# A transformer and state-space layer in float32 halves: the high and low parts of the activations side by side in memory, and one 512-column matmul for both

## The chip, the cores and the metric

The kernel runs on one core of a Trainium2 chip. The metric is the device time of one execution in microseconds (us), as the median of three runs. One further execution was recorded by the hardware profiler; all rows in this document that carry durations come from such recorded executions. TensorE (PE) does the matmuls, and its weight loads are listed apart (PEld); VectorE is DVE, ScalarE is ACT, SyncE (SP) issues nearly all transfers.

## The reference, cut to what matters

One layer for 256 tokens of width 1024, all in float32. Two feed-forward half steps enclose a mixer of latent attention and a state-space part:

```
x = x + 0.5 * swiglu(rmsnorm(x, ffn1_norm), w_gate1, w_up1, w_down1)     # inner width 2816
u = rmsnorm(x, mix_norm) @ w_in
c_q, c_kv, k_pe, z, xbc, dt_f, dt_b, g_a, g_b = split(u)
a = mla(c_q, c_kv, k_pe, ...)
m = bi_mamba2(xbc, z, dt_f, dt_b, ...)
merged = sigmoid(g_a) * (a @ w_attn_branch) + sigmoid(g_b) * (m @ w_ssm_branch)
x = x + merged @ w_out
x = x + 0.5 * swiglu(rmsnorm(x, ffn2_norm), w_gate2, w_up2, w_down2)

swiglu(h, wg, wu, wd) = (silu(h @ wg) * (h @ wu)) @ wd
```

## The kernel before, in words

Everything is kept transposed: 128 features on the partitions, the 256 tokens along the free dimension. A weight matrix is cut into tiles of 128 by 128; one such tile of the inner dimension is called a k-tile here.

**Three products for one.** Large products run on numbers of the reduced type fp32r, and accuracy is kept by splitting each operand into a high part and a low part: x = xh + xl, w = whi + wlo. `wstat` (line 140) goes over the k-tiles and calls `mm3` (lines 135 to 138) for each, which issues whi with xh, whi with xl and wlo with xh, all three into the same 256 PSUM columns. Each of these matmuls has a weight load of its own in the trace, so a k-tile takes three weight loads and three matmuls of 256 columns. The high parts and the low parts of the activations lie in separate tiles (`xh`, `xl`, `hh`, `hl`, `ah`, `al`, `mh`, `ml`, `oh`, `ol`).

**Weights.** `wload` (line 112) fetches a piece of up to 1088 columns into one of four raw buffers (pool `raw`), lets ACT make the high part by a copy (line 121 through line 94) and DVE the low part by a subtraction (line 122 through line 97), into one of four buffers each (pool `w`). The split carries a raised priority (`WPRI`). The order of instructions on each engine is laid down when the program is built, by a list scheduler that goes by such priorities and by its own estimate of when operands are there; the queues then run strictly in that order.

**Feed forward** (`ffn`, line 237). For each of 22 blocks f of the inner width, 1 MB of weights comes in as two pieces (gate and up), 16 k-tiles are multiplied into one PSUM bank, `gu` is the bank times the norm row R (line 264, DVE, straight from PSUM), ACT takes the silu of the gate half (266), DVE multiplies it with the up half (267), and `split` makes `hh` and `hl` of the result (268, one ACT and one DVE instruction). The PSUM pool has six one-bank buffers. Then come 8 down tiles d of 22 k-tiles each, with four pieces of weights; one DVE instruction (274) adds half of the 256 columns to x; `after(d)` feeds the next norm or, in the second half step, sends out a tile of the output. During blocks 8 to 18 of the first half step the hook also fetches and splits six pieces of the mixer's first weights, and during block 3 the rotary tables are made.

**Mixer.** Four rounds, in which the units of attention (`attn_group`), of the state-space part (`ssd_group`) and of weight-heavy filling are interleaved by a plan of keys (`put`). Filling is the input projection of the next group (`in_group`), in round 2 also `branch(0, c)` (first half of w_ssm_branch, copied to `mpb` by ACT), and in the last round `gates(c)`: 8 units, each two output tiles of 8 k-tiles in one PSUM bank, copied to `gt` by ACT. After the plan come the attention branch, `branch(1, c)` (added to `mpb` by DVE) and the output projection.

Of the kernel before, what the change touches and what calls it, by code (L numbers as in the profile page):

```python
# [15 lines left out]
P = 128  # L16
T = 256
# [6 lines left out]
# pool depths  # L24
# [48 lines left out]
def build(ctx, tc, A, out, dbg=None):  # L73
# [61 lines left out]
    def mm3(ps, whi, wlo, xhi, xlo, first, last):  # L135
        TE.matmul(ps, whi, xhi, start=first, stop=False)  # L136
        TE.matmul(ps, whi, xlo, start=False, stop=False)  # L137
        TE.matmul(ps, wlo, xhi, start=False, stop=last)  # L138

    def wstat(ps, pieces, xh, xl, k0, first, last):  # L140
        """ps[feature, token] += sum over the k tiles held in pieces"""
        ks = [(pc, j) for pc, j0, n in pieces for j in range(j0, j0 + n)]
        for i, (pc, j) in enumerate(ks):
            mm3(ps, pc.hi[:, j * P:(j + 1) * P], pc.lo[:, j * P:(j + 1) * P],
                xh[:, k0 + i], xl[:, k0 + i], first and i == 0, last and i == len(ks) - 1)

    def rsqrt(y, v, n):
        """y = v ** -0.5 on [P, n]"""
# [28 lines left out]
    def token_sums(psp, sq, tag):  # L177
        """[token, 2]: the sum of sq[feature, token] over its features"""
# [5 lines left out]
    def token_rows(psp, r, tag):  # L184
        """[P, token]: r[token, 2] on every partition"""
# [14 lines left out]
    def xn_tiles():  # L200
        xh = xnp.tile([P, KD, T], F32R, tag="xh", name="xh")
        xl = xnp.tile([P, KD, T], F32R, tag="xl", name="xl")
        return xh, xl

    class Norm:
        """x * gain of each tile of x as it comes, and the sum of squares"""

        def __init__(self, vcol):
            self.xh, self.xl = xn_tiles()
# [8 lines left out]
        def scale(self, k):  # L218
            g = vec[:, self.vcol + k:self.vcol + k + 1]
            split(self.xh[:, k], self.xl[:, k], x[:, k], g)  # L220
# [16 lines left out]
    def ffn(norm, wgu, wd, after, hook=None):  # L237
        with ExitStack() as es:
            hp = es.enter_context(pool("h", reuse_waits="tile"))
            ev = es.enter_context(pool("ev", 3, reuse_waits="tile"))  # L240
            ps_mm = es.enter_context(pool("ps_f", 6, space=PSUM, reuse_waits="tile"))
            ps_r = es.enter_context(pool("ps_fr", 2, space=PSUM, reuse_waits="tile"))
            hh = hp.tile([P, KF, T], F32R, name="hh")
            hl = hp.tile([P, KF, T], F32R, name="hl")
            R = None
            for f in range(KF):
                ps = ps_mm.tile([P, 2, T], F32, tag="mm", name="ps_gu")
                if f == 0 and hook:
# [4 lines left out]
                    for j in range(2):  # L253
                        wstat(ps[:, j], [(pcs[2 * j], 0, 4), (pcs[2 * j + 1], 0, 4)], norm.xh, norm.xl, 0, True, True)
# [9 lines left out]
                tt(gu, ps, R.unsqueeze(1).to_broadcast([P, 2, T]), ALU.mult)  # L264
# [3 lines left out]
                split(hh[:, f], hl[:, f], sg)  # L268
# [623 lines left out]
```

## Time and profile before

| what | us |
|---|---|
| three runs | 819.92, 818.7, 819.84 |
| median | 819.84 |
| span of the profiled execution | 817.6 |
| first half step, gate and up blocks | about 7 to 140 |
| first half step, down tiles | about 140 to 203 |
| mixer, branches, output projection | about 203 to 622 |
| second half step, gate and up blocks | about 622 to 752 |
| second half step, down tiles | about 752 to 817.6 |

The span runs from the first to the last instruction of the profiled execution; the median of the unprofiled runs lies 2.24 us above it. A matmul's listed duration is its whole way through the array, and matmuls overlap; what one costs in a row of them is the distance from its start to the next start. The granted TensorE clock was 1.00 throughout.

### The profile page before, as it was taken

The numbers are of one execution on the slowest core, as the hardware profiler recorded it, in microseconds if no ns is written. First come the engines' busy times: TensorE is split into PE (matmuls) and PEld (weight loads), VectorE is DVE, ScalarE is ACT, GpSimd is POOL, SyncE is SP. The second block draws the span as 40 slices with busy tenths as digits, with TensorE's granted clock in tenths as the row PEclk, the third lists the DMA queues.
The fourth block names the chain that finished last, engine by engine and source line by source line (L and its number), as shares of the span: only waits on it lengthen the run. The fifth ranks groups of instructions, "written<-read, shape, count | busy, mean of one in ns | idle before, by whom it ended". The sixth has DMA issues, their size and how long they took to land.

```text
span 817.6 us, 16082 instructions
## 1 busy us (share of the span) xinstructions
PE 797.8 (98%) x6480; PEld 768.8 (94%) x6480; DVE 590.3 (72%) x1192; ACT 470.2 (58%) x810; POOL 0.2 (0%) x4
## 2 busy tenths in 40 slices
PE   6999999999998999999999999999999999999998
PEld 5999999999998998988989999999999999999998
DVE  6977776566797986897897578657787766666543
ACT  6755554455367659679676666557455544444342
POOL 0000000000000000000000000000000000000000
PEclk9999999999999999999999999999999999999999
DMA  7667774667235443322325414342665555554772
GB/s 259 214 212 224 222 229 136 184 184 215 63 92 171 131 131 104 106 79 92 103 85 168 154 52 154 112 146 68 223 184 178 175 184 182 185 184 131 197 206 75
DMA packets 39098, 126.61 MB, mean 155 GB/s; under 512 B 4464, under 2 KB 5872, under 8 KB 39024
## 3 DMA queue, kind: packets, MB, share of 16 engines
q1 hardware_dynamic: 38592, 124.69, 48.7%
q8 instruction: 51, 0.84, 0.4%
q10 hardware_dynamic: 432, 0.89, 0.3%
q14 instruction: 23, 0.19, 0.1%
HBM read 124.52 MB, written 1.05 MB: 154 GB/s over the span
## 4 chain that ended last, share of the span: by engine, by line
PE 86%; DVE 6%; ACT 5%; DMA 2%; issue 1%; ACTq 0%
PE ps_gu L137 10%; PE ps_gu L138 10%; PE ps_gu L136 10%; PE ps_d L136 5%; PE ps_d L137 5%; PE ps_d L138 5%; PE ps_in L137 4%; PE ps_in L138 4%; PE ps_in L136 4%; PE ps_y L690 3%; PE ps_sb L138 2%; PE ps_sb L137 2%; PE ps_sb L136 2%; PE ps_sc L603 2%; PE ps_gt L137 1%; PE ps_o L630 1%
## 5 line engine op out<-in xcount | busy, mean ns | idle before, releaser
L94 ACT ACTIVATE whi<-raw 128x1024 fp32r<-128x1024 f32 (+4 forms) x256 | 251.3, 986 | 209.0 <-PE ps_d L137 53.1
L97 DVE TENSOR_TENSOR wlo<-raw,whi 128x1024 fp32r<-128x1024 f32 (+4 forms) x256 | 289.8, 1134 | 112.1 <-ACT whi L94 111.2
L136 PE MATMUL ps_gu<-xh,whi 128*128 128x256 f32 x704 | 201.0, 285 | 7.9 <-ACT whi L94 7.9
L137 PE MATMUL ps_gu<-xl,whi 128*128 128x256 f32 x704 | 201.2, 286 | 0.5 <-DVE xl L100 0.4
L138 PE MATMUL ps_gu<-xh,wlo 128*128 128x256 f32 x704 | 200.8, 285 | 0.0
L136 PEld LDWEIGHTS ps_gu<-xh,whi 128*128 128x128 f32 x704 | 136.5, 194 | 8.2 <-ACT whi L94 8.2
L137 PEld LDWEIGHTS ps_gu<-xl,whi 128*128 128x128 f32 x704 | 136.5, 194 | 1.0 <-DVE xl L100 0.9
L138 PEld LDWEIGHTS ps_gu<-xh,wlo 128*128 128x128 f32 x704 | 136.4, 194 | 0.5 <-DVE wlo L97 0.5
L137 PE MATMUL ps_in<-xl,whi 128*128 128x256 f32 x368 | 105.3, 286 | 0.1
L138 PE MATMUL ps_in<-xh,wlo 128*128 128x256 f32 x368 | 105.0, 285 | 0.0
L136 PE MATMUL ps_in<-xh,whi 128*128 128x256 f32 x368 | 104.4, 284 | 0.0
L137 PE MATMUL ps_d<-hl,whi 128*128 128x256 f32 x352 | 99.1, 281 | 0.0
L136 PE MATMUL ps_d<-hh,whi 128*128 128x256 f32 x352 | 99.1, 281 | 0.0
L138 PE MATMUL ps_d<-hh,wlo 128*128 128x256 f32 x352 | 99.0, 281 | 0.0
L137 PEld LDWEIGHTS ps_in<-xl,whi 128*128 128x128 f32 x368 | 70.1, 191 | 0.6 <-DVE xl L100 0.3
L138 PEld LDWEIGHTS ps_in<-xh,wlo 128*128 128x128 f32 x368 | 70.1, 191 | 0.5 <-issue 0.3
L136 PEld LDWEIGHTS ps_in<-xh,whi 128*128 128x128 f32 x368 | 70.1, 191 | 0.1
L136 PEld LDWEIGHTS ps_d<-hh,whi 128*128 128x128 f32 x352 | 66.3, 188 | 0.0
L137 PEld LDWEIGHTS ps_d<-hl,whi 128*128 128x128 f32 x352 | 66.3, 188 | 0.0
L138 PEld LDWEIGHTS ps_d<-hh,wlo 128*128 128x128 f32 x352 | 66.3, 188 | 0.0
L100 DVE SCALAR_TENSOR_TENSOR xz<-ps_in,vec,xz 128x254 f32<-128x254 f32 (+1 forms) x96 | 44.8, 476 | 1.6 <-ACT xz L520 0.9
L94 ACT ACTIVATE hh<-sg 128x256 fp32r<-128x256 f32 x44 | 18.1, 415 | 45.9 <-DVE sg L97 45.9
(222 smaller groups left out, 1467.5 us busy)
## 6 DMA issues: line engine op xcount, KB each, us to landing
raw<-in_w_gu SPq DMA_DIRECT2D x86, 512.0 KB, 4.5
raw<-in_w_in SPq DMA_DIRECT2D x62, 512.0 KB, 4.4
raw<-in_w_d SPq DMA_DIRECT2D x32, 384.0 KB, 3.2
raw<-in_w_d SPq DMA_DIRECT2D x32, 320.0 KB, 3.4
raw<-in_w_sb SPq DMA_DIRECT2D x16, 512.0 KB, 4.4
raw<-in_w_qkv SPq DMA_DIRECT2D x8, 544.0 KB, 3.8
raw<-in_w_ab SPq DMA_DIRECT2D x8, 512.0 KB, 3.8
raw<-in_w_o SPq DMA_DIRECT2D x8, 512.0 KB, 4.2
```

What stands on the lines that cost most here:

```text
L94: S.activation(dst, src, AF.Copy, scale=scale)
L97: V.tensor_tensor(out=dst, in0=a, in1=b, op=op)
L100: V.scalar_tensor_tensor(out=dst, in0=a, scalar=s, in1=b, op0=op0, op1=op1)
L136: TE.matmul(ps, whi, xhi, start=first, stop=False)
L137: TE.matmul(ps, whi, xlo, start=False, stop=False)
L138: TE.matmul(ps, wlo, xhi, start=False, stop=last)
L603: TE.matmul(sc[:, t * T:(t + 1) * T], qk[:HD, t * P:(t + 1) * P], qk[:HD, T:2 * T], start=True, stop=True)
L630: TE.matmul(po[64 * j:64 * j + 64, :T], kv[:, kt, HG * NOPE + hh_ * 64:HG * NOPE + (hh_ + 1) * 64], st[hh_][:, kt], start=kt == 0, stop=kt ...
L690: TE.matmul(py[64 * j:64 * j + 64, a:b], st[c, d][:, hh_], M[i][:, j, a:b], start=n == 0, stop=n == 3)
```

## The change

The high and the low part of an activation tile now lie side by side in one tile, `[P, K, 2, T]`, so that 512 neighbouring columns hold both (`xs`, `hs`, `as_`, `ms`, `os_`). A second function `wstat2` issues two matmuls for a k-tile: wlo with xh into the first 256 columns, and whi with both parts into all 512 columns. The products with xh (and wlo) thus gather in one half of a PSUM bank and the products of whi with xl in the other half, and the two halves are added afterwards. `wstat2` is used in both half steps (gate, up and down), in `gates` and in `branch(0, c)`. All other products keep `wstat` with three matmuls and only read the new layout.

The gate and up blocks get PSUM buffers of two banks, and the pool has three of them in place of six of one bank. The evacuation of a block is one ACT copy of the low halves, one DVE add from PSUM, and the multiplication by R, now from the copied tile. A down tile uses one bank of such a buffer, and x takes its two halves by two DVE instructions. `gates` and `branch(0, c)` use one bank for each output tile and add the halves with an ACT copy and a DVE add each. Comments were removed as well.

```diff
-    def mm3(ps, whi, wlo, xhi, xlo, first, last):
-        TE.matmul(ps, whi, xhi, start=first, stop=False)
-        TE.matmul(ps, whi, xlo, start=False, stop=False)
-        TE.matmul(ps, wlo, xhi, start=False, stop=last)
...
+    def wstat(ps, pieces, xs, k0, first, last):
+
         ks = [(pc, j) for pc, j0, n in pieces for j in range(j0, j0 + n)]
         for i, (pc, j) in enumerate(ks):
...
+            w = slice(j * P, (j + 1) * P)
+            xh, xl = xs[:, k0 + i, 0], xs[:, k0 + i, 1]
+            TE.matmul(ps, pc.hi[:, w], xh, start=first and i == 0, stop=False)
+            TE.matmul(ps, pc.hi[:, w], xl, start=False, stop=False)
+            TE.matmul(ps, pc.lo[:, w], xh, start=False, stop=last and i == len(ks) - 1)
+
+    def wstat2(ps, pieces, xs, k0, first, last):
+
+
+        ks = [(pc, j) for pc, j0, n in pieces for j in range(j0, j0 + n)]
+        for i, (pc, j) in enumerate(ks):
+            w = slice(j * P, (j + 1) * P)
+            a, b = first and i == 0, last and i == len(ks) - 1
+            if not a:
+                TE.matmul(ps[:, 0], pc.lo[:, w], xs[:, k0 + i, 0], start=False, stop=False)
+            TE.matmul(ps, pc.hi[:, w], xs[:, k0 + i], start=a, stop=b)
+            if a:
+                TE.matmul(ps[:, 0], pc.lo[:, w], xs[:, k0 + i, 0], start=False, stop=False)
...
     def xn_tiles():
-        xh = xnp.tile([P, KD, T], F32R, tag="xh", name="xh")
-        xl = xnp.tile([P, KD, T], F32R, tag="xl", name="xl")
-        return xh, xl
+        return xnp.tile([P, KD, 2, T], F32R, tag="xs", name="xs")
...
-            ps_mm = es.enter_context(pool("ps_f", 6, space=PSUM, reuse_waits="tile"))
+            ps_mm = es.enter_context(pool("ps_f", 3, space=PSUM, reuse_waits="tile"))
             ps_r = es.enter_context(pool("ps_fr", 2, space=PSUM, reuse_waits="tile"))
-            hh = hp.tile([P, KF, T], F32R, name="hh")
-            hl = hp.tile([P, KF, T], F32R, name="hl")
+            hs = hp.tile([P, KF, 2, T], F32R, name="hs")
             R = None
             for f in range(KF):
-                ps = ps_mm.tile([P, 2, T], F32, tag="mm", name="ps_gu")
+                ps = ps_mm.tile([P, 2, 2, T], F32, tag="mm", name="ps_gu")
...
-                        wstat(ps[:, j], [(pcs[j], 0, KD)], norm.xh, norm.xl, 0, True, True)
+                        wstat2(ps[:, j], [(pcs[j], 0, KD)], norm.xs, 0, True, True)
...
                 gu = ev.tile([P, 2, T], F32, tag="gu", name="gu")
-                tt(gu, ps, R.unsqueeze(1).to_broadcast([P, 2, T]), ALU.mult)
+                copy(gu, ps[:, :, 1])
+                tt(gu, ps[:, :, 0], gu, ALU.add)
+                tt(gu, gu, R.unsqueeze(1).to_broadcast([P, 2, T]), ALU.mult)
...
             for d in range(KD):
-                ps = ps_mm.tile([P, 2, T], F32, tag="mm", name="ps_d")
+                ps = ps_mm.tile([P, 2, 2, T], F32, tag="mm", name="ps_d")[:, 0]
                 for c in range(2):
                     pcs = wload(wd[d, c], [768, 640])
-                    wstat(ps[:, 0], [(pcs[0], 0, 6), (pcs[1], 0, 5)], hh, hl, 11 * c, c == 0, c == 1)
-                stt(x[:, d], ps[:, 0], 0.5, x[:, d], ALU.mult, ALU.add)
+                    wstat2(ps, [(pcs[0], 0, 6), (pcs[1], 0, 5)], hs, 11 * c, c == 0, c == 1)
+                for i in range(2):
+                    stt(x[:, d], ps[:, i], 0.5, x[:, d], ALU.mult, ALU.add)
                 after(d)
...
         def branch(b, c):
             pcs = wload(A["w_sb"][b, c], [1024, 1024])
+            if b == 0:
+                return halves(mpb[:, 2 * c:2 * c + 2], pcs, ms)
...
-            if b == 0:
-                copy(d, ps)
-            else:
-                tt(d, d, ps, ALU.add)
+            tt(d, d, ps, ALU.add)
+
+        def halves(dst, pcs, xs):
+            for j in range(2):
+                ps = ps_mm.tile([P, 2, T], F32, tag="mm", name="ps_half")
+                wstat2(ps, [(pcs[j], 0, 8)], xs, 0, True, True)
+                copy(dst[:, j], ps[:, 1])
+                tt(dst[:, j], ps[:, 0], dst[:, j], ALU.add)
...
         def gates(c):
             gt[c] = ss.tile([P, 2, T], F32, tag="xz", name="gt", bufs=10)
             pcs = wload(A["w_in2"][c], [1024, 1024])
-            ps = ps_mm.tile([P, 2, T], F32, tag="mm", name="ps_gt")
-            for j in range(2):
-                wstat(ps[:, j], [(pcs[j], 0, KD)], xh, xl, 0, True, True)
-            copy(gt[c], ps)
+            halves(gt[c], pcs, xs)
```

More of the change, by code (lines that the diff above doesn't have):

```diff
@@ L133, in split @@
             stt(lo, src, scale, hi, ALU.mult, ALU.subtract)
-    def mm3(ps, whi, wlo, xhi, xlo, first, last):
[L136 to L140, printed above, removed]
+    def wstat(ps, pieces, xs, k0, first, last):
         ks = [(pc, j) for pc, j0, n in pieces for j in range(j0, j0 + n)]
         for i, (pc, j) in enumerate(ks):
-            mm3(ps, pc.hi[:, j * P:(j + 1) * P], pc.lo[:, j * P:(j + 1) * P],
-                xh[:, k0 + i], xl[:, k0 + i], first and i == 0, last and i == len(ks) - 1)
+            w = slice(j * P, (j + 1) * P)
[13 more added lines that the diff above has]
+                TE.matmul(ps[:, 0], pc.lo[:, w], xs[:, k0 + i, 0], start=False, stop=False)
     def rsqrt(y, v, n):
@@ L253, in ffn @@
                     for j in range(2):
-                        wstat(ps[:, j], [(pcs[2 * j], 0, 4), (pcs[2 * j + 1], 0, 4)], norm.xh, norm.xl, 0, True, True)
+                        wstat2(ps[:, j], [(pcs[2 * j], 0, 4), (pcs[2 * j + 1], 0, 4)], norm.xs, 0, True, True)
                 else:
@@ L396, in build @@
         ss = es.enter_context(pool("ssd", reuse_waits="tile", side="right"))
-        xh, xl = xn_tiles()
+        xs = xn_tiles()
         for k in range(KD):
@@ L494, in build @@
         dump("acs", acs)
-        ah, al = xn_tiles()
-        mh = mp.tile([P, 8, T], F32R, name="mh")
-        ml = mp.tile([P, 8, T], F32R, name="ml")
+        as_ = xn_tiles()
+        ms = mp.tile([P, 8, 2, T], F32R, name="ms")
         mpb = mp.tile([P, 8, T], F32, name="mpb")
```

26 lines of the change are left out of this document (13 added, 13 removed).

## The prediction

> **What bounds the kernel now.** I read the page first: shares of the engines, chain of waits, costliest groups.
>
> ```profile
> span 817.6 us, 16082 instructions
> ...
> PE 797.8 (98%) x6480; PEld 768.8 (94%) x6480; DVE 590.3 (72%) x1192; ACT 470.2 (58%) x810; POOL 0.2 (0%) x4
> ...
> PE 86%; DVE 6%; ACT 5%; DMA 2%; issue 1%; ACTq 0%
> ...
> L136 PE MATMUL ps_gu<-xh,whi 128*128 128x256 f32 x704 | 201.0, 285 | 7.9 <-ACT whi L94 7.9
> ...
> L136 PEld LDWEIGHTS ps_gu<-xh,whi 128*128 128x128 f32 x704 | 136.5, 194 | 8.2 <-ACT whi L94 8.2
> ```
>
> The chain that ended last runs over PE for 86% of the span, and there are as many weight loads as matmuls. The listed 285 ns is a matmul's whole way through the array: 6480 of them would make 1847 us, so matmuls overlap. What counts is the distance between starts. The windows by stage give it:
>
> ```profile
> 7.00:32.00 25.00, 24.05 (x163) 22.89 (x164) 22.77 (x75) 17.82 (x32) 0.00 (x0) 1.00 0.82 274
> 32.00:90.00 58.00, 58.00 (x486) 58.00 (x485) 44.97 (x61) 34.58 (x50) 0.00 (x0) 1.00 0.64 206
> 90.00:140.00 50.00, 50.00 (x419) 50.00 (x418) 35.50 (x47) 25.58 (x37) 0.00 (x0) 1.00 0.64 197
> 140.00:202.60 62.60, 62.60 (x530) 62.60 (x529) 38.06 (x55) 31.80 (x48) 0.00 (x0) 1.00 0.66 191
> 450.00:485.00 35.00, 34.98 (x282) 32.12 (x282) 20.04 (x54) 24.28 (x55) 0.00 (x0) 1.00 0.31 101
> 634.00:700.00 66.00, 66.00 (x552) 65.97 (x551) 45.25 (x60) 32.87 (x49) 0.00 (x0) 1.00 0.56 180
> 700.00:752.00 52.00, 52.00 (x435) 52.00 (x435) 34.35 (x46) 24.22 (x37) 0.00 (x0) 1.00 0.55 166
> ```
>
> Columns: length, then busy time and count of PE, PEld, DVE, ACT, POOL, then clock, DMA share, GB/s. In the second half step's gate and up blocks a matmul starts every 66.00/552 = 119.6 ns, in the down tiles every 62.60/530 = 118.1 ns, without a gap. PE sets the pace there, at the full clock. In the first 25 us it does not: 163 matmuls need 153 ns each, and DVE is busy 22.77 of the 25 us.
>
> **What a k-tile costs, before and after.** Why 119.6 ns for 256 columns? Three other shapes, from the PE timeline:
>
> ```profile
> 26.18 0.61 PE L181 MATMUL ps_sum<-ones,nacc 128*128 128x1 f32 x4
> 26.64 0.36 PE L137 MATMUL ps_gu<-xl,whi 128*128 128x256 f32 x1
> ...
> 255.41 0.28 PE L555 MATMUL ps_qkv<-whi,cql 128*128 128x192 f32 x1
> 255.52 0.31 PE L558 MATMUL ps_qkv<-whi,ckh 128*128 128x256 f32 x1
> ...
> 351.55 1.03 PE L646 MATMUL ps_cb<-xz 128*128 128x256 f32 x4
> 352.41 1.04 PE L654 MATMUL ps_xT<-cst,xz 128*128 128x128 f32 x8
> 353.29 0.29 PE L597 MATMUL ps_qkT<-cst,qs 128*96 128x128 f32 x1
> ```
>
> One-column matmuls with a 128-column weight load start every 0.46/4 = 115 ns, 192-column ones after 0.11 us, the 128-column transposes every 0.88/8 = 110 ns. Below 192 columns the length of the matmul does not matter: the weight load of about 110 ns does. At 256 columns load and stream are about equal, and together cost 119.6. The row ps_cb is the other case: full float32 operands, 0.86/4 = 215 ns for 256 columns, hence a matmul twice as long under which its weight load vanishes.
>
> After the change a k-tile is one 256-column matmul, under which the next (high) weights are loaded, and one 512-column matmul, under which the next low weights are loaded. The first is today's pair: 119.6 ns (118.1 in the down tiles). No 512-column matmul is in the trace. The nearest rows bound it: 215 ns from ps_cb, and 2 x 119.6 = 239 ns if the columns themselves, not the load, made 119.6. I take 216, since at 192 columns the stream was still hidden in 110 ns and ps_cb shows a long stream losing nothing to its load. So a k-tile goes from 3 x 119.6 = 358.8 to 335.6 ns, 23.2 saved; in the down tiles from 354.3 to 334.1, 20.2 saved.
>
> The Trainium skill, page "TensorE: Matmul & The Clock Gate", section "Back-to-back issue gap", speaks for another value: it states a sustained 81 ns per matmul for 128 columns and 131 ns for 512, with weight loads pipelined between. Here 128 columns took 110 ns, so its first figure does not hold in this trace. By its second a k-tile would be an estimated 251 ns and the change worth five times as much; it is the last rival below.
>
> **Part by part**, as savings against the 817.6 us span.
>
> *Down tiles.* 2 x 8 x 22 = 352 k-tiles x 20.2 ns = 7.1 us. DVE is busy 38.06 of 62.60 us there; eight more additions are covered by its idle time.
>
> *Gate and up, second half step.* 352 k-tiles x 23.2 = 8.2 us, if DVE keeps up: PE's block of 16 k-tiles goes from 5.74 to 5.37 us. What is added to a block, by the nearest groups:
>
> ```profile
> L97 DVE TENSOR_TENSOR gu<-ps_gu,R 128x512 f32<-128x512 f32 x44 | 30.2, 689 | 17.2 <-PE ps_gu L138 17.2
> L97 DVE TENSOR_TENSOR E<-E,cb 128x512 f32<-128x512 f32 x48 | 32.1, 686 | 1.8 <-ACT E L681 1.4
> L94 ACT ACTIVATE gt<-ps_gt 128x512 f32<-128x512 f32 x8 | 4.7, 588 | 0.1
> L100 DVE SCALAR_TENSOR_TENSOR x<-ps_d,x 128x256 f32<-128x256 f32 x16 | 6.8, 424 | 6.8 <-PE ps_d L138 6.4
> L97 DVE TENSOR_TENSOR yg<-yg,xz 128x256 f32<-128x256 f32 x16 | 6.7, 418 | 0.1
> ```
>
> The add takes the place of today's multiplication from PSUM (689 ns); the multiplication from SBUF is new on DVE (like E<-E,cb, 686 ns) and the copy is new on ACT (like gt<-ps_gt, 588 ns). How DVE works through a block when it need not wait for PE:
>
> ```profile
> 89.61 0.68 DVE L97 TENSOR_TENSOR gu<-ps_gu,R 128x512 f32<-128x512 f32 x1
> 90.21 1.22 DVE L97 TENSOR_TENSOR wlo<-raw,whi 128x1024 fp32r<-128x1024 f32 x1
> 91.34 0.42 DVE L97 TENSOR_TENSOR sg<-sg,gu 128x256 f32<-128x256 f32 x1
> 92.25 0.42 DVE L97 TENSOR_TENSOR hl<-sg,hh 128x256 fp32r<-128x256 f32 x1 [0.48 <-ACT hh L94]
> 93.20 1.22 DVE L97 TENSOR_TENSOR wlo<-raw,whi 128x1024 fp32r<-128x1024 f32 x1 [0.53 <-ACT whi L94]
> 94.34 0.68 DVE L97 TENSOR_TENSOR gu<-ps_gu,R 128x512 f32<-128x512 f32 x1
> ```
>
> Start to start 94.34 - 89.61 = 4.73 us, of which 1.01 are waits for ACT. The new multiplication adds 0.60 (gu to the next start, 90.21 - 89.61): 5.33 us, against PE's 5.37. If other work fills the waits it is 4.32; if DVE also waits out the copy each time, 4.73 + 0.60 + 0.59 = 5.92. Since ACT has the room (32.87 busy of 66.00, plus 0.59 a block), and a block waits for nothing that PE holds back for over one block (four weight buffers, three PSUM buffers), I take the 5.33: it just fits. Saving 7.8 of the 8.2. Should DVE lag, its queue holds behind the waiting add the next wlo and so PE's weights.
>
> *Gate and up, first half step.* The same 8.2, but DVE has more to do here. Busy 22.77 + 44.97 + 35.50 = 103.2 us in 133; 22 new multiplications make it 116.4, while PE could be done in 124.8. That leaves 8.4 us for waits; at 1.01 for the 17 blocks after the start there are 17. Ends: nothing lost (8.2), or all waits kept (116.4 + 17 + 2.2 of the start = 135.6, 2.6 slower than now). In the first 25 us, 163/3 = 54 k-tiles, nothing is to be gained (1.3 us). The order is laid out anew, and where DVE is late more work lies ready to fill a wait, so I go a little above the middle: 3.0 saved.
>
> *Mixer.* gates: 8 x 16 = 128 k-tiles x 23.2 = 3.0 us; branch(0, c): 4 x 16 = 64 x 23.2 = 1.5. Each of the 24 output tiles adds a DVE addition of 0.42 (yg row), and the ACT copy is cut in two; in 450 to 485 DVE is busy 20.04 of 35 us and ACT 24.28, which covers it. Attention and state-space units cross these stages, so I take 3.5, ends 2 and 4.5.
>
> *Ends.* After the last matmul two additions stand in line for x where there was one: 0.4 us at the end of the kernel, and 0.4 before the mixer's first norm tile, which PE waits for (0 if hidden). Lost: 0.8.
>
> *Nothing for the rest.* Weight bytes are the same; 1 MB per 5.37 us is 195 GB/s, and the first window moved 274. Three PSUM pairs hold a block each, and a pair is free about 1.3 us (copy and add) after its last matmul, two blocks before it is needed. Other products keep their three matmuls.
>
> Sum: 7.1 + 7.8 + 3.0 + 3.5 - 0.8 = 20.6 us. Span 797.0; the runs' median is 819.84, 2.24 above the span, and I carry that along: **799.2 us**.
>
> **Rivals.**
>
> *DVE takes over the gate and up blocks* (the other side). The copy stands on ACT behind other work, DVE waits it out, and a block takes 5.92 in place of 5.74: 44 x 0.18 = 7.9 us lost, and the six prefetched pieces (1.13 of DVE each, 90.21 to 91.34) no longer fit beside PE, 6.8 more. Against it 7.1 + 3.5 - 0.8 = 9.8 saved elsewhere: 819.84 + 14.7 - 9.8 = 824.7. For it speaks that 5.33 is only 0.04 below PE's pace; against it that ACT is half idle. It loses on the whole when 44 x (c - 5.74) + 6.8 exceeds 9.8, at a block time c above 5.81. Chance 3 in 100. Between 5.37 and 5.81 it eats part of the gain: at 5.55, 44 x 0.18 = 7.9 lost of the 10.8 that the gate and up blocks were to give, about 807. Chance 10.
>
> *The columns, not the loads, made 119.6.* A 512-column matmul takes 239 ns, or is carried out as two of 256 with a load each, so that the change does not do what it says. PE gains nothing; 0.8 at the ends and about 1.5 of the DVE work in the first half step are lost: 822. For it: 256 columns cost 10 ns more than 192. Against it: ps_cb. Chance 5, of which 2 come out within 0.2%.
>
> *In between*, 512 columns with the same 10 ns on top: 226 ns. 1248 k-tiles (352 + 352 + 352 + 192) x 10 = 12.5 us less, of which some 2 come back since DVE has more time: about 810. Chance 9.
>
> *Long matmuls overlap*: a 512-column one costs no more than today's 256. Then 119.6 fall away for each k-tile: down tiles 42 us; in gate and up DVE binds at 5.33, 44 x 0.41 = 18 at most less the first half step's 5; mixer perhaps 15. About 70 us saved, 750. Nothing in the trace supports it, ps_cb speaks against it. Chance 3. The Trainium skill's figure above would be this case.
>
> **How the numbers follow.** The forecast has 70 in 100. Its own range: all of the terms at their good ends give 7.1 + 8.2 + 8.2 + 4.5 = 28.0, 792; a weight load under a short matmul that costs 110 rather than 119.6, now that every second one has room, would give a few more, 789. At their bad ends (first half step 2.6 lost, mixer 2) the sum is 7.1 + 7.0 - 2.6 + 2.0 - 0.8 = 12.7, 807. The range also takes in the in-between cases at 807 and 810: 789 to 811. About 0.2% (1.6 us) is what a measurement of this kernel can tell from no change. Faster 70 + 10 + 9 + 3 = 92, same 2, slower 3 + 3 = 6.
>
> **What would show it.** In the changed profile: a down-tile stage (now 62.6 us) of about 59; 22 x 16 matmuls fewer per half step's gate and up blocks, as many weight loads fewer; starts 0.12 and 0.22 us apart in turn; gate and up in the second half step some 8 us shorter with DVE above 80% busy; PE waiting for wlo in the first half step for a few us. I am wrong if the long start-to-start is above 0.23, if PE's waits for wlo (DVE) or whi reach 10 us, or if a block's DVE cycle exceeds 5.4.

## The result and the profile after

The changed kernel takes **810.07 us** (median of four runs, 808.55 to 811.59), the kernel before 819.88 beside it: a ratio of 0.988 with a 95% interval of 0.9857 to 0.9903. That is 9.8 us faster, where 20.6 were forecast; the time lies just inside the forecast's range. The page of the profiled execution after:

```profile
span 808.1 us, 13739 instructions
...
PE 786.8 (97%) x5232; PEld 700.4 (87%) x5232; DVE 625.0 (77%) x1276; ACT 493.6 (61%) x866; POOL 0.2 (0%) x4
...
PE 87%; DVE 6%; ACT 5%; issue 1%; DMA 1%; ACTq 0%
...
L154 PE MATMUL ps_gu<-xs,whi 128*128 128x512 f32 x704 | 243.8, 400 | 7.8 <-DVE xs L100 7.7
L153 PE MATMUL ps_gu<-xs,wlo 128*128 128x256 f32 x616 | 173.3, 281 | 1.8 <-DVE wlo L97 1.8
```

The change does what it says: 6480 - 5232 = 1248 matmuls and as many weight loads are gone, one for each k-tile, and none of the long ones is carried out as two. PE still carries 87% of the chain that ended last. The windows, with the columns of those before (length, busy time and count of PE, PEld, DVE, ACT, POOL, clock, DMA share, GB/s), of the stretches 7 to 32 and 32 to 90 us (first half step), 140 to 198 (down tiles) and 634 to 740 (second half step's gate and up blocks):

```profile
7.00:32.00 25.00, 22.93 (x113) 19.41 (x114) 21.98 (x64) 16.97 (x31) 0.00 (x0) 1.00 0.79 268
32.00:90.00 58.00, 57.72 (x330) 50.09 (x329) 52.08 (x86) 41.12 (x64) 0.00 (x0) 1.00 0.64 209
140.00:198.00 58.00, 58.00 (x333) 50.87 (x332) 37.84 (x60) 30.96 (x47) 0.00 (x0) 1.00 0.67 196
634.00:740.00 106.00, 106.00 (x608) 92.33 (x607) 84.35 (x115) 62.34 (x96) 0.00 (x0) 1.00 0.57 182
```

A k-tile is now two matmuls: 58.00 / 333 x 2 = 348.3 ns in the down tiles, 106.00 / 608 x 2 = 348.7 ns in the gate and up blocks. Before, it was three: 354.3 and 358.8. A window also counts the one or two matmuls under way at its left edge, so all four values (and the prediction's 118.1 and 119.6 a matmul) are a little low: from start to start a k-tile takes 350 and 349 ns now, and took 356 and 360. The differences stay. So 6 and 10 ns are saved, not 20.2 and 23.2, and PE has no gap in either stretch: nothing else holds it up. By stage in the two traces, gate and up and down tiles each from the stage's first matmul's start to its last's, the mixer from the last down matmul's start to the first of the second half step:

| stage | before | after | saving forecast | saving measured |
|---|---|---|---|---|
| gate and up, first half step | 132.45 | 129.66 | 3.0 | 2.8 |
| down tiles, first | 62.54 | 61.41 | 3.55 | 1.1 |
| mixer, up to the second half step | 419.82 | 418.67 | 3.1 | 1.15 |
| gate and up, second half step | 128.91 | 125.10 | 7.8 | 3.8 |
| down tiles, second | 62.54 | 61.42 | 3.55 | 1.1 |
| after the last matmul's start | 3.73 | 4.09 | -0.4 | -0.4 |

The rest (the first matmul 0.1 earlier, the steps between the stages 0.2 longer) brings the sum to the 9.5 us by which the spans differ. The shares are where the forecast has them, at a third to a half of the size, except at the start.

The first row has a scatter of its own. Up to the end of that stage *after_again*, *mix_three* and *mix_grouped* (below) run the change's instructions in the same order on PE, DVE and ACT, and take 129.73, 128.54 and 128.24 us for it. From the 201st matmul on all four take the same 87.87 us; before it, the matmuls run at about half pace at first, until 16.2 us in the change, 17.0, 14.8 and 11.6 in the other three. A difference of 1.5 us at the start can thus not be put down to a difference between two kernels.

PE's timeline in the second half step, as start, duration, instruction:

```profile
660.04 0.28 PE L153 MATMUL ps_gu<-xs,wlo 128*128 128x256 f32 x1
660.16 0.39 PE L154 MATMUL ps_gu<-xs,whi 128*128 128x512 f32 x1
660.39 0.27 PE L153 MATMUL ps_gu<-xs,wlo 128*128 128x256 f32 x1
660.50 0.40 PE L154 MATMUL ps_gu<-xs,whi 128*128 128x512 f32 x1
660.73 0.28 PE L153 MATMUL ps_gu<-xs,wlo 128*128 128x256 f32 x1
```

The short matmul holds the place for 0.11 to 0.12 us, as forecast, the long one for 0.23 (0.39 - 0.16, 0.73 - 0.50) in place of 0.216. Was it DVE that slowed PE down? One block's cycle on DVE in the same stage; the brackets give the idle time ahead of an instruction and what ended it:

```profile
693.04 0.69 DVE L97 TENSOR_TENSOR gu<-ps_gu,gu 128x512 f32<-128x512 f32 x1 [0.74 <-ACT gu L94]
...
698.64 0.69 DVE L97 TENSOR_TENSOR gu<-ps_gu,gu 128x512 f32<-128x512 f32 x1 [0.75 <-ACT gu L94]
```

698.64 - 693.04 = 5.60 us, more than the 5.4 that the prediction set as a sign against itself. But the block of 16 k-tiles takes PE 16 x 349.4 = 5.59, and the copy whose end DVE waits for is itself waiting for PE's last matmul (in the trace, ACT's copy into gu waits for ps_gu in 18 of the 20 blocks after 634 us). DVE follows PE here; the experiment with less evacuation, below, tests that.

### The profile page after: what moved, and what is told of

The parts are those of the page before. It is cut to its first block, busy times and chain, and to the rows that moved or that the text cites. A ratio compares the mean times of both kernels' runs of the same rounds, so it can differ in the third digit from the quotient of the medians.

```text
span 808.1 us, 13739 instructions
## 1 busy us (share of the span) xinstructions
PE 786.8 (97%) x5232; PEld 700.4 (87%) x5232; DVE 625.0 (77%) x1276; ACT 493.6 (61%) x866; POOL 0.2 (0%) x4
## 4 chain that ended last, share of the span: by engine, by line
PE 87%; DVE 6%; ACT 5%; issue 1%; DMA 1%; ACTq 0%
PE ps_gu L154 20%; PE ps_d L154 10%; PE ps_gu L153 9%; PE ps_half L154 5%; PE ps_d L153 5%; PE ps_in L142 4%; PE ps_in L143 4%; PE ps_in L141 4%; PE ps_y L700 3%; PE ps_half L153 2%; PE ps_sc L613 2%; PE ps_o L640 1%; PE ps_gu L156 1%; PE ps_pl L682 1%; DVE wlo L97 1%; PE ps_pT L630 1%
## 5 line engine op out<-in xcount | busy, mean ns | idle before, releaser
L154 PE MATMUL ps_gu<-xs,whi 128*128 128x512 f32 x704 | 243.8, 400 | 7.8 <-DVE xs L100 7.7
L153 PE MATMUL ps_gu<-xs,wlo 128*128 128x256 f32 x616 | 173.3, 281 | 1.8 <-DVE wlo L97 1.8
L154 PEld LDWEIGHTS ps_gu<-xs,whi 128*128 128x128 f32 x704 | 127.2, 190 | 32.2 <-ACT whi L94 7.2
L153 PEld LDWEIGHTS ps_gu<-xs,wlo 128*128 128x128 f32 x616 | 117.4, 191 | 6.4 <-DVE wlo L97 2.3
L154 PE MATMUL ps_d<-hs,whi 128*128 128x512 f32 x352 | 122.5, 393 | 0.0
L142 PE MATMUL ps_in<-xs,whi 128*128 128x256 f32 x368 | 105.3, 286 | 0.6 <-DVE xs L100 0.6
L143 PE MATMUL ps_in<-xs,wlo 128*128 128x256 f32 x368 | 105.0, 285 | 0.0
L141 PE MATMUL ps_in<-xs,whi 128*128 128x256 f32 x368 | 104.3, 283 | 0.0
L153 PE MATMUL ps_d<-hs,wlo 128*128 128x256 f32 x336 | 94.7, 282 | 0.0
L142 PEld LDWEIGHTS ps_in<-xs,whi 128*128 128x128 f32 x368 | 70.1, 190 | 1.2 <-DVE xs L100 0.8
L143 PEld LDWEIGHTS ps_in<-xs,wlo 128*128 128x128 f32 x368 | 70.1, 191 | 0.5 <-issue 0.3
L141 PEld LDWEIGHTS ps_in<-xs,whi 128*128 128x128 f32 x368 | 70.1, 190 | 0.1
```

Of the source, the lines that this page charges most:

```text
L141: TE.matmul(ps, pc.hi[:, w], xh, start=first and i == 0, stop=False)
L142: TE.matmul(ps, pc.hi[:, w], xl, start=False, stop=False)
L143: TE.matmul(ps, pc.lo[:, w], xh, start=False, stop=last and i == len(ks) - 1)
L153: TE.matmul(ps[:, 0], pc.lo[:, w], xs[:, k0 + i, 0], start=False, stop=False)
L154: TE.matmul(ps, pc.hi[:, w], xs[:, k0 + i], start=a, stop=b)
```

## The experiments

The question is where the other 11 us went. The theories: 512 columns of this reduced type simply take longer than 216 ns (A); a weight load does not hide under a matmul (B); transfers and the other engines' traffic slow the stream (C); accumulation in one bank does (D); after the first measurements also that a change of length from matmul to matmul costs something (E), or a change of the weight tile (F). For the layer as a whole the rival is that the evacuation on ACT and DVE holds PE up.

**Two measurements of the matmul by itself.** They share one kernel, which computes nothing of the layer; it runs rows of 64 matmuls of one shape, and the second fetches and splits 88 weight pieces beside them.

```diff
+    def run(name, n, w, mv, reps, m=P, alone=False, step=512):
+        ps = bank(name)
+        for r in range(reps):
+            k = r % 8
+            TE.matmul(ps[:m, :n], w[:, k * P:k * P + m], mv[:, k * step:k * step + n],
+                      start=alone or r == 0, stop=alone or r == reps - 1)
+        finish(ps, m)
...
+    run("ps_rc", 256, hi, xsf, 64)
...
+    run("ps_rg", 512, hi, xsf, 64)
+    run("ps_halfw", 512, hi, xsf, 64, m=64)
...
+    run("ps_full", 256, wf, xf, 64, step=256)
...
+    run("ps_bg", 512, wb, xbf, 64)
```

Quiet:

> Only the start of the layer is kept (x split, one piece of weights); then rows of matmuls of one form each, with ACT, DVE and the queues idle, one weight load each: fp32r of 128 to 512 columns, 512 and 256 with weights half as wide (64 columns), 512 without accumulation, the pair 256 low / 512 high in one bank and in two banks, full float32 of 256 columns, bf16 of 256 and 512. The layer's output is not computed. Theory A, the fp32r columns themselves cost about 0.45 ns at full clock: 512 columns start every 230 to 233 ns, 384 every 172 to 175, half-wide weights change nothing at 512 (230 to 233), bf16 512 takes 214 to 218. Theory B, the weight load disturbs the stream: half-wide weights bring 512 columns to about 222, and bf16 512 is disturbed too (over 222). Theory C, writes of ACT, DVE and transfers into the memory from which TensorE reads disturb it: here, in quiet, 512 takes 214 to 218. Theory D, adding into the bank just written: without accumulation, and with the pair in two banks, 512 takes 214 to 218.

With the traffic:

> The same rows of matmuls while 88 pieces of weights are fetched and split beside them (the matmuls do not use them). Theories A, B and D: the starts are within 3 ns of those in quiet. Theory C: 512 columns of fp32r go to 230 ns or more here and are at 214 to 218 in quiet.

The quiet kernel took 220.04 us in all, the busy one 221.26. PE's timeline of the quiet one; each line is a row of 64, so the distance to the next line's start, divided by 64, is the price of one:

```profile
32.78 7.34 PE L228 MATMUL ps_rb<-xs,whi_k 128*128 128x192 f32 x64
39.95 7.86 PE L228 MATMUL ps_rc<-xs,whi_k 128*128 128x256 f32 x64
47.65 9.55 PE L228 MATMUL ps_rd<-xs,whi_k 128*128 128x320 f32 x64
57.04 11.26 PE L228 MATMUL ps_re<-xs,whi_k 128*128 128x384 f32 x64
68.14 13.38 PE L228 MATMUL ps_rf<-xs,whi_k 128*128 128x448 f32 x64
81.36 14.71 PE L228 MATMUL ps_rg<-xs,whi_k 128*128 128x512 f32 x64
95.91 14.88 PE L228 MATMUL ps_halfw<-xs,whi_k 128*64 128x512 f32 x64
110.62 7.44 PE L228 MATMUL ps_halfwc<-xs,whi_k 128*64 128x256 f32 x64
117.90 14.70 PE L228 MATMUL ps_alone<-xs,whi_k 128*128 128x512 f32 x64
...
166.22 27.79 PE L228 MATMUL ps_full<-x,wf_k 128*128 128x256 f32 x128
193.85 7.15 PE L228 MATMUL ps_bc<-xb,wb_k 128*128 128x256 bf16 x64
200.84 13.98 PE L228 MATMUL ps_bg<-xb,wb_k 128*128 128x512 bf16 x64
```

Of the reduced type, 192 columns take 7.17/64 = 112 ns, 256 take 120, 320 147, 384 173, 448 207 and 512 (95.91 - 81.36)/64 = **227**. In bf16, 256 columns take 6.99/64 = 109, and the 64 matmuls of 512 columns start 216 ns apart. So 512 columns do go in at 216 in bf16; the reduced type takes 11 ns more there as well as at 256 columns. A weight load of half the width (ps_halfw) doesn't bring 512 columns down (230), but takes 256 (ps_halfwc) to 114, some half of the way to bf16; without accumulation (ps_alone) 512 are at 227 as well, and the pair in two banks takes 353 as in one. The weight loads beside these rows, listed at 192 ns each for ps_rc, are shorter in two of them:

```profile
L228 PEld LDWEIGHTS ps_halfwc<-xs,whi_k 128*64 128x64 f32 x64 | 7.3, 134 | 0.2
L228 PEld LDWEIGHTS <-wb_k 128*128 128x128 bf16 x128 | 12.5, 98 | 8.2
```

At 256 columns the price follows the listed length of the load (192, 134, 98 ns: 120, 114, 109), so there the load can have its part in it; at 512 it doesn't (230 with the short load).

And the row ps_full shows what the prediction's row ps_cb was: 64 matmuls on full float32 appear as 128 records. A record of 215 ns there is one of two for a matmul of 256 columns, and says nothing about how fast 512 columns of the reduced type go in. (Of the prediction's other rows, ps_sum and ps_xT are full float32 with two records a matmul too, 2 and 4 matmuls behind the 4 and 8 records; the floor of about 110 ns that it read from them is there in the reduced type all the same, 111 at 128 columns and 112 at 192.) The busy kernel has the same prices to within 0.5 ns; its stretch of 40 to 96 us moved 258 GB/s:

```profile
40.00:96.00 56.00, 56.00 (x328) 52.48 (x327) 34.42 (x32) 28.90 (x28) 0.00 (x0) 1.00 0.80 258
```

C and D fall, and B falls at 512 columns. A holds there in its core: the price lies in the form itself. Why it has one (how the operands reach the array) no run shows.

The Trainium skill, page "TensorE: Matmul & The Clock Gate", section "Back-to-back issue gap", gives for a single matmul columns/2.4 + 2.5 ns, an estimate of 109 at 256 and 216 at 512: the bf16 rows agree, the reduced type's don't. Its sustained 131 ns for 512 columns, a rival in the prediction, holds in neither (216 and 227).

**In which order.** 227 + 120 = 347 is what a k-tile should cost, and the layer has 349 to 350 from start to start. But in the quiet kernel the pair of a k-tile, in turn, takes 353: 237 and 117. Rows of 32 k-tiles (ps_od 64), with the 512-column (high) and 256-column (low) matmuls in different groups:

```diff
+    order("ps_oa", [H + (None,), L + (None,)], 32)
+    order("ps_ob", [H + (0,), H + (1,), L + (0,), L + (1,)], 16)
+    order("ps_oc", [H + (k,) for k in range(4)] + [L + (k,) for k in range(4)], 8)
+    order("ps_od", [H + (k,) for k in range(8)] + [L + (k,) for k in range(8)], 8)
+    order("ps_oe", [(False, 512, None), (True, 512, None)], 32)
...
+    order("ps_og", [(False, 512, None), (False, 256, None)], 32)
```

> Rows of matmuls by themselves again (the layer's output is not computed), now in the order of the change and in others. In quiet an even row of fp32r matmuls started every columns/2.4 + 13.4 ns (120 for 256, 227 for 512), the alternation of 512 high and 256 low every 236.7 and 116.7, together 353. Theory E, changing the length from one matmul to the next costs the extra 6 ns: high and low weights in turn at 512 columns each stay at 227 (row oe), 512 and 256 from the same weights cost 353 (row og), two and two about 350 (ob), four and four 348 (oc), eight and eight 347 to 348 a pair (od). Theory F, switching between the tiles of high and low weights costs it: oe is at 232 or more, og at 347. bf16 in alternation of 512 and 256 (row oj): 216 + 109 = 325, if the cost is fp32r's.

PE's timeline, the first matmul of each row:

```profile
25.30 0.39 PE L239 MATMUL ps_oa<-xs,whi_k 128*128 128x512 f32 x1
...
36.59 0.40 PE L239 MATMUL ps_ob<-xs,whi_k 128*128 128x512 f32 x1
...
47.75 0.40 PE L239 MATMUL ps_oc<-xs,whi_k 128*128 128x512 f32 x1
...
58.98 0.40 PE L239 MATMUL ps_od<-xs,whi_k 128*128 128x512 f32 x1
...
81.32 0.40 PE L239 MATMUL ps_oe<-xs,whi_k 128*128 128x512 f32 x1
...
95.86 0.28 PE L239 MATMUL ps_of<-xs,whi_k 128*128 128x256 f32 x1
...
103.53 0.40 PE L239 MATMUL ps_og<-xs,whi_k 128*128 128x512 f32 x1
...
114.84 0.40 PE L239 MATMUL ps_oh<-xs,whi_k 128*128 128x512 f32 x1
```

In turn 11.29/32 = 352.8 ns a k-tile, two and two 348.8, four and four 350.9, eight and eight 22.34/64 = 349.1. With one length throughout, high and low weights in turn cost nothing extra (ps_oe 14.54/64 = 227.2), so F falls. Different lengths in turn with the same high weights (ps_og) cost 11.31/32 = 353.4. So in this kernel the extra comes with the change of length, as E has it; grouping regains 4 ns of 353, and in the layer, which is at 349 to 350 already, there may be nothing to regain. That E holds in the layer isn't shown: *hi_first*, below, changes length at every matmul and has a k-tile at 353.6 ns in one stage and at 346.7 in another, and in *grouped* the long matmuls take 231 ns on average although they stand next to each other. What sets the extra stays open.

**Parts of the change.** Four kernels shared a chip and the runs of the kernel before (819.37 us):

| kernel | median us | ratio, 95% interval |
|---|---|---|
| down_only: only the down tiles changed | 818.14 | 0.9985 (0.9976 to 0.9994) |
| mix_three: all but gates and first branch changed | 809.74 | 0.9885 (0.9872 to 0.9899) |
| evac_light: whole change, lighter evacuation | 813.78 | 0.9931 (0.9919 to 0.9944) |
| hi_first: whole change, high before low | 807.72 | 0.9860 (0.9847 to 0.9874) |

*down_only* puts the gate and up blocks, their evacuation, the six one-bank buffers, gates and the first branch back:

```diff
-                        wstat2(ps[:, j], [(pcs[j], 0, KD)], norm.xs, 0, True, True)
+                        wstat(ps[:, j], [(pcs[j], 0, KD)], norm.xs, 0, True, True)
...
-                copy(gu, ps[:, :, 1])
-                tt(gu, ps[:, :, 0], gu, ALU.add)
-                tt(gu, gu, R.unsqueeze(1).to_broadcast([P, 2, T]), ALU.mult)
+                tt(gu, ps, R.unsqueeze(1).to_broadcast([P, 2, T]), ALU.mult)
```

> Only the down tiles of both half steps use the 512-column matmul; gate, up, gates and branch have three matmuls and their old evacuation. If a 512-column matmul costs 232 ns wherever it stands, a down k-tile saves 4 to 6 ns: 352 of them 1.4 to 2.3 us, less 0.8 at the ends, so 0.5 to 1.5 us faster than before, with the down stage at 61.4 us in place of 62.5. If the loss in the whole change came from DVE and ACT in gate and up, the down tiles alone give the forecast 7.1 - 0.8 = 6.3 us.

1.2 us were gained. Its window in the down tiles:

```profile
141.00:201.00 60.00, 60.00 (x344) 52.56 (x343) 38.55 (x61) 31.37 (x48) 0.00 (x0) 1.00 0.66 193
```

60.00/344 x 2 = 348.8 ns, within 1 ns of the whole change's 348.3 by the same count. The part alone is worth what the stage table says, less what the longer ends take.

*mix_three* puts only gates and the first branch back:

```diff
...
-            halves(gt[c], pcs, xs)
+            ps = ps_mm.tile([P, 2, T], F32, tag="mm", name="ps_gt")
+            for j in range(2):
+                wstat(ps[:, j], [(pcs[j], 0, KD)], xs, 0, True, True)
+            copy(gt[c], ps)
```

> The change with gates and branch(0, c) put back to three matmuls. If each of their 192 k-tiles saves about 9 ns, this is 1.3 to 1.8 us slower than the whole change, that is 8 us faster than before. If the mixer's share was lost to its extra copies and additions: within 0.5 us of the whole change.

No difference to the whole change can be measured by the medians. In the traces the mixer takes 419.61 us in place of 418.67, and the first gate and up stage, which doesn't contain them, 1.1 less. 192 k-tiles x 10 ns = 1.9 was the most that could have come from the part; 0.9 is left of it in the mixer.

*evac_light* takes the copy and the addition away; the multiplication reads PSUM again. It leaves out the products of high weights with low activations in gate and up:

```diff
-                copy(gu, ps[:, :, 1])
-                tt(gu, ps[:, :, 0], gu, ALU.add)
-                tt(gu, gu, R.unsqueeze(1).to_broadcast([P, 2, T]), ALU.mult)
+                tt(gu, ps[:, :, 0], R.unsqueeze(1).to_broadcast([P, 2, T]), ALU.mult)
```

> The whole change, but the copy and the addition of the gate and up blocks are left out: gu is the first half of the pair times R, and the products of the high weights with the low activations are lost there. If DVE and ACT set the pace of these blocks, this is 5 us or more faster than the whole change. If TensorE sets it with 350 ns a k-tile and DVE matters at the start alone: 0 to 1 us faster than the whole change, 10 to 11 faster than before.

It came out 3.7 us *slower* than the whole change, which neither theory expected. Its window in the second half step:

```profile
634.00:740.00 106.00, 106.00 (x609) 92.35 (x608) 74.33 (x98) 53.13 (x79) 0.00 (x0) 1.00 0.55 182
```

DVE is busy 10.0 us less there and ACT 9.2, and PE starts 609 matmuls in place of 608. The evacuation costs nothing in that stage: that PE's own pace sets the time there is shown. The loss lies at the start (first gate and up stage 133.61 against 129.66, more than the scatter found there). PE's timeline there:

```profile
31.30 0.70 PE L201 MATMUL ps_rows<-diag,ones 128*128 128x256 f32 x2 [1.36 <-DVE diag L104]
...
33.20 0.79 PE L154 MATMUL ps_gu<-xs,whi 128*128 128x512 f32 x1 [1.20 <-DVE gu L97]
...
34.22 0.63 PE L154 MATMUL ps_gu<-xs,whi 128*128 128x512 f32 x1
34.64 0.41 PE L153 MATMUL ps_gu<-xs,wlo 128*128 128x256 f32 x1
```

The row R is made from a sum over all of x; the first multiplication by it starts at 32.5 us here, and at 35.8 us in the change. Where the evacuation begins with R, three blocks (96 matmuls) fill the three buffer pairs and PE must wait (1.36 and 1.20 us); then it runs at half pace for two microseconds (34.22 to 34.64 for 512 columns: 0.42), with a granted clock of 0.50 from 34 to 36 us. The change's copy and add don't need R: they free the first three pairs by 19.9, 25.4 and 31.8 us, and only the multiplication waits. The prediction had booked these two instructions as a burden alone.

*hi_first* issues the high matmul first in every k-tile:

```diff
-            if not a:
-                TE.matmul(ps[:, 0], pc.lo[:, w], xs[:, k0 + i, 0], start=False, stop=False)
-            TE.matmul(ps, pc.hi[:, w], xs[:, k0 + i], start=a, stop=b)
-            if a:
-                TE.matmul(ps[:, 0], pc.lo[:, w], xs[:, k0 + i, 0], start=False, stop=False)
+            TE.matmul(ps, pc.hi[:, w], xs[:, k0 + i], start=a, stop=False)
+            TE.matmul(ps[:, 0], pc.lo[:, w], xs[:, k0 + i, 0], start=False, stop=b)
```

> The whole change, but in each k-tile the high weights come first, 512 columns, then the low ones. In a running row the sequence is the same, so no stage inside changes. At the start of the layer TensorE's fifth k-tile no longer waits for the low half of the second piece (12.21 us in place of 11.17): about 1 us faster than the whole change if that wait costs what it shows, no difference if the next wait takes its place.

2.4 us better by the medians, though the intervals of the two ratios overlap (0.9847 to 0.9874 here, 0.9857 to 0.9903 for the change). Its profile doesn't put the gain at the start (first gate and up stage 130.38): the second takes 124.27 and the mixer 417.74, 0.8 and 0.9 less than in the change. That no stage inside would change was expected, and it does. Two windows of it, in the first and the second half step's gate and up blocks:

```profile
60.00:130.00 70.00, 70.00 (x398) 60.67 (x397) 61.34 (x81) 45.44 (x68) 0.00 (x0) 1.00 0.68 220
640.00:735.00 95.00, 95.00 (x551) 83.77 (x550) 77.26 (x104) 56.99 (x87) 0.00 (x0) 1.00 0.57 185
```

From start to start a k-tile takes 353.6 ns in the first and 346.7 in the second, against 349.3 in both for the change. The same matmuls in the same order differ by 7 ns a k-tile from one half step to the other, so the order alone doesn't set the pace; what does isn't known.

**Grouping in the layer.** All high matmuls of a piece, then all low ones, wherever the change uses `wstat2`; in *grouped_all* the 512-column form is also taken, grouped, into products that the change left with three matmuls: the z part of the input projection, the attention branch, the second half of w_ssm_branch and the output projection. *after_again* is the changed kernel once more, on the same chip:

```diff
-        ks = [(pc, j) for pc, j0, n in pieces for j in range(j0, j0 + n)]
-        for i, (pc, j) in enumerate(ks):
...
+        for pc, j0, n in pieces:
+            for j in range(n):
+                w = slice((j0 + j) * P, (j0 + j + 1) * P)
+                TE.matmul(ps, pc.hi[:, w], xs[:, k0 + i + j], start=first and i + j == 0, stop=False)
+            for j in range(n):
+                w = slice((j0 + j) * P, (j0 + j + 1) * P)
+                TE.matmul(ps[:, 0], pc.lo[:, w], xs[:, k0 + i + j, 0], start=False, stop=last and i + j == n_all - 1)
+            i += n
```

> The whole change, but the matmuls of a piece of weights are issued as all the 512-column ones and then all the 256-column ones. Theory E: a k-tile goes from 350 to 347 or 348, 1248 times: 2.5 to 4 us faster than the whole change, and at the start of the layer about 1 us more, since the low weights are needed later. If the order within a piece does not matter: only the start, 0 to 1 us.

> As grouped, and the 512-column matmul also in the z part of the input projection, the attention branch, the second half of w_ssm_branch and the output projection (320 k-tiles more), with their halves added by more DVE and ACT work. At 10 to 13 ns a k-tile 3 to 4 us faster than grouped; if DVE (busy 47 of 59 us in the branches) becomes late there, no faster or slower than grouped.

> The change as it is, beside the others on the same chip: 809 to 811 us.

| kernel | median us | ratio, 95% interval |
|---|---|---|
| after_again | 810.12 | 0.9890 (0.9877 to 0.9903) |
| grouped | 805.38 | 0.9833 (0.9820 to 0.9845) |
| grouped_all | 823.52 | 1.0047 (1.0035 to 1.0059) |

The kernel before took 819.33 beside them. *grouped* beats both kernels, the change by 4.7 us. But not by a better pace. Its windows in the down tiles and the second half step:

```profile
137.00:195.00 58.00, 58.00 (x332) 50.61 (x331) 38.27 (x61) 30.05 (x47) 0.00 (x0) 1.00 0.67 196
634.00:735.00 101.00, 101.00 (x581) 88.94 (x581) 81.31 (x110) 60.15 (x92) 0.00 (x0) 1.00 0.55 182
```

58.00/332 x 2 = 349.4 and 101.00/581 x 2 = 347.7 ns: the change had 348.3 and 348.7. In the traces the gain lies at the start (first gate and up stage 127.19 against 129.66) and in the mixer (415.76 against 418.75 in after_again). Of the part at the start most may be scatter: *grouped_all* issues the same matmuls in the same order up to there and takes 128.77, and half pace ends at 13.3 us in *grouped*, at 16.0 in *grouped_all*. At the start, the changed kernel's PE, and that of grouped:

```profile
12.21 0.58 PE L153 MATMUL ps_gu<-xs,wlo 128*128 128x256 f32 x1 [1.83 <-DVE wlo L97]
12.59 0.63 PE L154 MATMUL ps_gu<-xs,whi 128*128 128x512 f32 x1
13.02 0.41 PE L153 MATMUL ps_gu<-xs,wlo 128*128 128x256 f32 x1
13.23 0.63 PE L154 MATMUL ps_gu<-xs,whi 128*128 128x512 f32 x1
```

```profile
11.08 2.07 PE L152 MATMUL ps_gu<-xs,whi 128*128 128x512 f32 x4
12.95 0.77 PE L155 MATMUL ps_gu<-xs,wlo 128*128 128x256 f32 x4
```

With the low matmul first PE waits 1.83 us for the low weights, which DVE makes from the high ones; grouped has the high matmuls of four k-tiles to do meanwhile (x4 in its rows).

*grouped_all* is slower than the kernel before. Its mixer takes 432.21 us. What PE waits for there, as total, times, longest:

```profile
PE ps_pT L634 <- DVE pr L104: 8.8, 6, 4.0
PE ps_gu L152 <- DVE x L97: 3.7, 1, 3.7
PE ps_half L152 <- DVE abt L97: 2.8, 1, 2.8
```

```profile
345.00:360.00 15.00, 12.77 (x80) 9.66 (x79) 12.62 (x26) 7.13 (x17) 0.00 (x0) 0.89 0.20 72
563.00:632.00 69.00, 61.64 (x345) 53.27 (x344) 61.82 (x117) 36.38 (x56) 0.00 (x0) 0.99 0.56 183
```

The waits that took the place of the saving are put down to DVE: busy 12.62 of 15.00 us around the longest and 61.82 of 69.00 at the mixer's end, where each output tile has an addition more. And after the waits the clock falls (0.89 granted in the stretch around the longest). The rival in which DVE takes over was wrong for the half steps, and by this profile is right for the mixer if the change is carried on into it; no run takes the additions away to show it.

**Which part of the grouping pays.** Grouped order in the first half step's first block only, and in `halves` (gates and first branch) only (`wstat3` is the grouped order):

```diff
-                        wstat2(ps[:, j], [(pcs[2 * j], 0, 4), (pcs[2 * j + 1], 0, 4)], norm.xs, 0, True, True)
+                        wstat3(ps[:, j], [(pcs[2 * j], 0, 4), (pcs[2 * j + 1], 0, 4)], norm.xs, 0, True, True)
...
-                wstat2(ps, [(pcs[j], 0, 8)], xs, 0, True, True)
+                wstat3(ps, [(pcs[j], 0, 8)], xs, 0, True, True)
```

> The whole change, but the first block of the first half step alone is issued as grouped does: all 512-column matmuls of a piece, then all 256-column ones. If the gain of grouped over the whole change (4.7 us) comes mostly from the start of the layer, where the low weights are late: 2 to 3 us faster than the whole change, 807 to 808. If it comes from the order in running rows: no difference.

> The whole change, but in gates and branch(0, c) alone the matmuls are issued as grouped does. If the rest of its gain lies in the mixer, whose stages from the last group's scores to the attention branch were 2 us shorter in grouped: 1.5 to 2.5 us faster than the whole change, 807.5 to 808.5. If it lies only at the start: no difference.

The first gave 809.58 us, 0.9871 (0.9849 to 0.9893), not to be told from the change: PE's wait for low weights is gone, another of 1.13 us for the activations stands there, and the first gate and up stage takes 128.96 us, within the scatter; the second 807.13, 0.9840 (0.9826 to 0.9855), 3 better (before: 819.89). By the medians most of grouped's gain is the mixer's, where the stretch from the last state-space group (its first ps_cb matmul) to the attention branch takes 41.22 us in place of 43.51. The scheduler lays the mixer's order out anew when `halves` changes, PE's listed waits in the mixer fall by less than 1 us (those for pr from 1.7 to 0.8), and what is behind the rest wasn't taken apart.

## Why the prediction was right in its direction and wrong in its size

*What bounds the kernel*: right. PE at the pace of its matmuls, before and after, in the down tiles and the second half step without a gap.

*A k-tile*: this is the step that failed. "I take 216, since at 192 columns the stream was still hidden in 110 ns and ps_cb shows a long stream losing nothing to its load." The sum's largest terms rest on it. Measured: 227 alone and 230 to 234 beside a short matmul, so that a k-tile takes about 349 ns in the gate and up blocks and 350 in the down tiles, not 335.6 and 334.1. The sign that the prediction had named against itself, a long start-to-start above 0.23, was there. The reason given falls with it: the 10 ns above the floor at 256 columns were taken for load and stream together, gone once the stream is long. At 256 columns the load may well have its part (half of it, 114), but a price of 11 ns over bf16 is there at 512 columns as well, where half the load takes nothing off. The row ps_cb was no bound from below: its record is one of two for a matmul of another type. The mechanism holds (one matmul and one load less), at half its size: 704 k-tiles of gate and up save 10 ns where 23.2 stood, 352 of the down tiles 6 where 20.2 stood.

*Down tiles* 7.1: measured 2.2, by that term alone; the added instructions were covered, as booked. *Second half step* 7.8: measured 3.8, by that term alone. DVE's cycle of 5.60 us, a sign named against the forecast, misled: it follows PE's block. *Mixer* 3.5: measured 1.15 with the 0.4 at the stage's head in it, and 0.9 of it by putting the part back. *Ends* -0.8: the last stretch lost 0.4, as booked.

*First half step* 3.0: measured 2.8 (and up to 4.2, by the scatter of the start), but not as reasoned: that the number was met is luck. From 32 to 90 us PE is busy 57.72 of 58.00, so DVE held back no more than 0.3 there. The 113 matmuls up to 32 us are some 56 k-tiles; the other 296 saved 10 ns each, 3.0, and in this trace the start gave nothing. In it the copy and add that were booked as DVE's burden also free the buffers before R is known, which evac_light shows by losing some 4 us of this stage without them; against it stands the low weights' wait of 1.83.

*The rivals*: "in between", 226 ns and about 810, is nearly what came; it had 9 in 100, and its reason, the same 10 ns on top at 512 columns, is what the quiet kernel measured (227). The forecast's range took in this case, so that the time lies inside it says nothing for the 216. DVE taking over the gate and up blocks didn't come, and evac_light shows it isn't near. Of "the columns, not the loads" half is right: at 512 columns it isn't the load that makes the price, but a matmul of 512 pays it once, not twice. Long matmuls that overlap didn't come: 512 columns take 227 ns, nearly twice 120.

## What to carry to other kernels

Before a duration is multiplied by 1248, it must come from the same number type and the same length; a row of another type is no bound, and a record may be one of two for a matmul. Two traces of the same instructions can differ by 1.5 us at the start, so a gain of that size in one stage needs more than one trace. An extra evacuation step that doesn't need the late factor can pay by freeing its buffer early. Whether an order of matmuls is better shows only in the whole kernel: grouping gained 4.7 us here with the k-tiles' price within 1 ns of the change's, and the long form taken into more of the mixer lost more than all of it.

## What the runs showed of the hardware

The reduced type lies 11 ns above bf16 at 256 columns (120, 109) and at 512 (227, 216), and 17 above the straight line between those two at 448 (207, 189). A 512-column matmul next to a 256-column one costs 237 + 117 in the quiet kernel, 6 ns over the two alone; in the layer the same alternation took 346.7 to 353.6 a pair, by stage (hi_first). A 256-column matmul on full float32 appears as two records of 216 ns.

The first matmuls, from 7 us on, run at about half pace: 512 columns 0.43 us, 256 columns 0.21 (12.59, 13.02, 13.23 in the changed kernel), while the granted clock of these windows reads 1.00. This ended between 11.6 us (mix_grouped) and 17.2 us (hi_first). Half pace came again in evac_light for two microseconds after waits of 1.36 and 1.20 us, and there the granted clock reads 0.50. The Trainium skill, page "TensorE: Matmul & The Clock Gate", section "Back-to-back issue gap", gives columns/1.2 ns for the cold array, an estimate of 427 and 213: these rows agree, so by that rule the reduced type pays nothing on top at that pace.
